# Gate products 6, 7 and 4 moved out of the attention heads into one PSUM bank per column behind them

## The chip, the core and the metric

The kernel runs on one core of a Trainium2 chip. A core has a matrix engine (PE, its weight loads shown as PEld), a vector engine (DVE), a scalar engine (ACT), GpSimd (POOL), a queue engine (SP), and 16 DMA engines which they all feed. Matmuls write to PSUM, eight banks of 128 partitions x 512 floats; everything else works in SBUF. The metric is the device time in microseconds of one execution; lower is better.

## The reference

One layer of an encoder on a sequence of 1024 tokens of width 1024, in float32:

```
h     = rmsnorm(x) * g_mix
z     = h @ w_in                         # 512 pooling channels | q | k | v
y_pool = pool_mixer(z[:, :512])          # windows 2, 4, 8, 16; per-group 128x128 map
y_attn = diff_attention(q, k, v)         # 8 heads, two softmax maps each
gates  = sigmoid(h @ w_gate + b_gate)    # 1024 x 2048
merged = gates[:, :1024] * (y_pool @ w_branch_pool) + gates[:, 1024:] * (y_attn @ w_branch_attn)
x = x + merged @ w_out
x = x + square(relu(rmsnorm(x) * g_ffn @ w_up)) @ w_down
```

The change concerns `h @ w_gate`: where its matmuls run, and how their results reach memory.

## The kernel before

**Exact float32 from split operands.** Each operand of a matmul is split into a high part (an ACT cast, line 136) and a low part (a subtraction on DVE or POOL, line 137). `mm3` (lines 140 to 145) multiplies high x high, high x low and low x high into one bank, so every product is three matmuls.

**Stages.** Setup and the norm of x; then the heads (a loop over `g`, lines 1024 to 1049); then the rest of the gates; then the pooling branch (`bp`, `branch_pool`), the attention branch (`ba`), `w_out` (`oX`, `oY`, `oZ`), and the MLP.

**The heads.** A turn `g` handles one tile of 128 tokens in each of nine stages, each some turns behind the one before (`ORDER`): A is q, k and v (`z`, 24 matmuls of 384 columns), B their norms, C the transposes of q and k (`tk`), D the scores, exponentials and the weighted difference (`sc`, `s`, `cf`), E the transpose of the probabilities (`ta`, `AT`), F the product with v (`po`), H and R the output norm, W the next head's weights. There are 64 tiles, 8 for each of 8 heads, and `g` runs on for ten more turns while the last stages drain.

**The fillers.** Matmuls that don't depend on the heads are mixed in as fillers. `fillers()` (line 489) walks through `G_PLAN` (line 51) and yields after each piece with its size in units. Line 1048 calls it until `made` reaches `F_UNITS` = 62 or `(g - 4) * 1.03`. What is left is issued behind the loop (line 1051). The pieces are:
- U, a pooling group: `h @ w_in` for 128 channels (`u`), the trailing sums on DVE, and the group's map (`yp`).
- A, B, 6, 4, 7: the gates.
- tB, t6, t4, t7: `t_set`, which prepares the second operands of products 5, 6, 4 and 7.
- A dot: an empty unit.

**The gates as Strassen's products.** `h @ w_gate` is cut into quarters and computed in Winograd's form of Strassen's algorithm, with seven products instead of eight. A product is done for one of eight blocks of 128 columns at a time: 4 blocks of the inner dimension x 3 matmuls of 512 columns, 12 matmuls. Its first operand is a column block of `w_gate` or of a sum of its quarters (`gw_sum`, made in memory by `gate_sums` with copies and accumulating DMAs at the turns of `G_SUMS`). Its second is a half of the transposed `h` (products 1, 2, 3) or a sum of quarters of it (`T`, products 5, 6, 7, 4). A piece A does products 1 and 2 in one bank, B does 5 and 3, and 6, 4, 7 are single.

`gate_unit` (line 465) loads the weights (`gate_weights`: a raw tile `frg` of a pool of two, split into `fwg`), does the matmuls, copies the bank with ACT after each product (`go`, lines 478 and 480) and sends the copy to those of the four quarters of `gd[c]` that it belongs to (`G_TO`). Products 1 and 2 are stored from ACT's queue (line 485); the others are added by an accumulating DMA from POOL's queue (line 487). Later `gate()` (line 236) loads the quarters for the sigmoid.

`t_set` (line 418) loads the two quarters of `h` (lines 435 and 436), subtracts on DVE (line 437) and splits into four tiles `T`. All four sets share the same four tiles; the fifth product's differences are also stored (`t2_dram`), and an accumulating DMA turns them into the operand of product 6.

**What sets the order.** The program states the order of its instructions; a scheduler of the language orders each engine's queue from it by priority and a modelled timeline when the kernel is built, within the tile slots that are free. At run time each queue is worked off in that order. `tc.issue_after(ins)` puts instructions behind `ins` on its engine.

**Room.** `ps_f` has one bank (`fill_bank`); behind the loop the gates take one of three (`spare_bank`). `up` has 11 slots `U`, which hold K, V, the scores and the probabilities, and later operands `yT` of the attention branch. `hp0` holds the first half of the transposed `h` (`hT`), `hp1` the second; `wpool` the heads' weights.

Of the kernel before, what the change touches and what calls it, by code (L numbers as in the profile page):

```python
# [49 lines left out]
F_FROM, F_PACE, F_UNITS = 4, 1.03, 62  # L50
G_PLAN = "A A A U A U A U A U A A . tB B B B B B B B B . t6 6 6 6 6 6 6 6 6 . t4 4 4 4 4 4 4 4 4 . t7 7 7 7 7 7 7 7 7"
G_SUMS = {
    9: "h0", 10: "i0 c1", 11: "h1", 12: "i1 a10", 13: "a11", 14: "h2", 15: "i2 c2", 16: "h3", 17: "i3 c3", 18: "a20",
    19: "a21", 20: "h4", 21: "i4 a30", 22: "a31", 23: "h5", 24: "i5 c4", 25: "h6", 26: "i6 a40", 27: "a41", 28: "h7", 29: "i7",
}
G_TO = {"1": (1, 4), "2": (0, 1), "6": (1, 4), "7": (2, 4), "5": (2, 3), "3": (1, 2), "4": (3, 4)}
# [12 lines left out]
def encoder_kernel(  # L69
# [248 lines left out]
    def fill_w(src, c0, name):  # L318
        ws = []
        for j in range(2):  # L320
            rw = fr_tile([P, 4, P], f"fr{name}_{j}")
            nc.sync.dma_start(
                rw, src[j * 512 : (j + 1) * 512, c0 : c0 + P].rearrange("(kk p) c -> p kk c", p=P)
            )
            w = fw_tile([P, 2, 4, P], f"fw{name}_{j}")
            split(w[:, 0], w[:, 1], rw, nc.gpsimd)
            ws.append(w)
        return ws

# [21 lines left out]
    def pool_group(g):  # L351
        win = WINDOWS[g]
        ws = fill_w(w_in, g * P, f"pool{g}")
        rg = fr_tile([P, P], f"rgrp{g}")
        nc.sync.dma_start(rg, w_pool_grp[g])
        wg = fq.tile([P, 2, P], F32R, tag="wg", name=f"wgrp{g}")
        split(wg[:, 0, :], wg[:, 1, :], rg, nc.gpsimd)
        u = fu_tile(f"u{g}")
        for th in range(2):
# [23 lines left out]
            split(m[:, 0, :], m[:, 1, :], cur[:, n0:n])  # L383
            yield
# [6 lines left out]
    def gate_sums(what):  # L391
# [14 lines left out]
        elif what[0] == "c":  # L406
            src = (None, wq(1, 0), gw_sum["1"], wq(1, 0), gw_sum["2"])[n]
            with tc.issue_after(marks["SP"]):
                nc.sync.dma_start(gw_sum[what[1]], src)
        else:  # L410
            src = (None, wq(1, 1), wq(0, 0), wq(0, 0), wq(0, 1))[n]
            r = slice(int(what[2]) * 256, int(what[2]) * 256 + 256)
            with tc.issue_after(marks["POOL"]):
                nc.gpsimd.dma_start(gw_sum[what[1]][r, :], src[r, :], accum_op=ALU.add, max_dma_last_dim=1024)
# [3 lines left out]
    def t_set(j):  # L418

        for k in range(4):  # L420
            if k < 2:
                t = fq.tile([P, 2, 512], F32R, tag=("fu", "mx")[k], name=f"T{j}_{k}")
            else:
                t = fwpool.tile([P, 2, 512], F32R, tag="fT", name=f"T{j}_{k}", bufs=N_FW // 2)
            T[j, k] = t
            rows = slice(k * P, (k + 1) * P)
            rw = raw([P, S], f"rT{j}_{k}")
            a, b = rw[:, 0:512], rw[:, 512:S]
            if j == "6":
                nc.sync.dma_start(a, t2_dram[rows, :])  # L430
            else:
                sa, sb = {
                    "5": (h_dram[0][0], h_dram[0][1]), "7": (h_dram[1][1], h_dram[0][1]), "4": (t2_dram, h_dram[1][0]),
                }[j]
                nc.sync.dma_start(a, sa[rows, :])
                nc.sync.dma_start(b, sb[rows, :])
                nc.vector.tensor_tensor(a, a, b, op=ALU.subtract)
            if j == "5":
                nc.sync.dma_start(t2_dram[rows, :], a)
            split(t[:, 0, :], t[:, 1, :], a)  # L440
        if j == "5":
            nc.gpsimd.dma_start(t2_dram, h_dram[1][1], accum_op=ALU.add, max_dma_last_dim=1024)
# [3 lines left out]
    def gate_weights(j, c):  # L446
# [8 lines left out]
        rw = fr_tile([P, 4, P], f"frg{j}_{c}")  # L455
        with ExitStack() as later:
            if n < 6:
                later.enter_context(tc.issue_after(h_hi[n // 2 + 2].ins))
                later.enter_context(tc.issue_after(loads["x3"].ins))
            marks["SP"] = nc.sync.dma_start(rw, src[r0 : r0 + 512, c0 : c0 + P].rearrange("(kk p) c -> p kk c", p=P)).ins  # L460
            w = fw_tile([P, 2, 4, P], f"fwg{j}_{c}")
            split(w[:, 0], w[:, 1], rw, nc.gpsimd)
        return w

    def gate_unit(js, c):

        ws = [gate_weights(j, c) for j in js]
        ps = (spare_bank if in_tail[0] else fill_bank)(f"g{js}_{c}")
        for n, (j, w) in enumerate(zip(js, ws)):
            for k in range(4):  # L470
                if j in "123":
                    b = [hT[k // 2 + 2 * (j != "1"), int(j == "3"), hl][:, k % 2, :] for hl in range(2)]
                else:
                    b = pair(T[j, k])
                mm3(ps, w[:, 0, k, :], w[:, 1, k, :], *b, k == 0 and n == 0, k == 3, n > 0)
            fo = fo_tile(f"go{j}_{c}")
            if j == "6":
                nc.scalar.activation(fo[:, 0:512], ps, AF.Copy, scale=-1.0)
            else:
                nc.scalar.copy(fo[:, 0:512], ps)  # L480
# [3 lines left out]
            if j in "12":  # L484
                nc.scalar.dma_start(dst, from_)
            else:
                nc.gpsimd.dma_start(dst, from_, accum_op=ALU.add)  # L487
# [1239 lines left out]
```

## Time and profile before

| | |
|---|---|
| median of 3 runs | 1548.94 us (1548.9 to 1551.23) |
| the profiled execution | 1553.23 us, of which the span from first to last instruction is 1551.5 us |
| granted PE clock over the span | 0.992 |
| instructions | 21873 |
| matmuls | 7542 |

Times below are from one profiled execution. A group is a line of the kernel, an engine, an operation, output <- inputs by their names without buffer numbers, and a count; behind it stand the busy time, the mean of one in ns, and the engine's idle time ahead of it with what ended that. PE's busy times come from matmuls whose ends are modelled. The chain that ended last can be followed back only to 823.8 us, where it begins with an instruction whose release the profile doesn't show; so for the heads and the gates PE's idle times and their releasers are used, and not this chain.

The page's slices show where the stages lie. Each digit is the busy share of one fortieth of the span, 38.8 us, in tenths:

```profile
PE   9999999999999999979999999999999999999999
POOL 4435355442636353445966420000000000000000
PEclk9999999999999999989999999999999999999999
DMA  7867687262434467589963733545442789637650
```

The heads fill the first 17 slices, the eighteenth and nineteenth hold the end of the heads and the remaining gates.

### The profile page before, as it was taken

How to read it: one execution, taken by the hardware profiler on the slowest of the kernel's cores; microseconds unless marked ns; L12 is line 12 of the kernel's file. 1: busy time of each engine (PE TensorE's matmuls, PEld its weight loads, DVE VectorE, ACT ScalarE, POOL GpSimd, SP SyncE). 2: the span in 40 equal slices, each digit the busy share in tenths (PEclk: the TensorE clock that was granted, in tenths of full speed). 3: DMA queues.
4: the chain of work that ended last, by engine and by line, in shares of the span. 5: the costliest groups of instructions: out<-in, count | busy, mean ns of one | idle time of the engine just before them, and what ended most of it. 6: DMA issues, size and time to landing. Idle time of an engine off the chain costs nothing. (4 is left out here: it accounts for less than half of the span.)

```text
span 1551.5 us, 21873 instructions
## 1 busy us (share of the span) xinstructions
PE 1516.4 (98%) x7542; PEld 1303.3 (84%) x7542; DVE 1069.1 (69%) x2101; ACT 829.2 (53%) x1717; POOL 460.5 (30%) x484
## 2 busy tenths in 40 slices
PE   9999999999999999979999999999999999999999
PEld 8899898989898989857888787888888878888887
DVE  7677767776867767764764799776666578546672
ACT  7666566565656656653553368566555544333331
POOL 4435355442636353445966420000000000000000
PEclk9999999999999999989999999999999999999999
DMA  7867687262434467589963733545442789637650
GB/s 228 295 115 218 138 170 142 71 201 71 107 62 96 86 147 139 134 214 280 360 210 121 260 143 101 164 165 188 150 142 109 255 314 367 217 122 256 225 191 27
DMA packets 210457, 271.43 MB, mean 175 GB/s; under 512 B 12037, under 2 KB 127466, under 8 KB 210282
## 3 DMA queue, kind: packets, MB, share of 16 engines
q1 hardware_dynamic: 172810, 212.32, 41.3%
q0 software_dynamic: 20368, 30.41, 13.4%
q10 hardware_dynamic: 17168, 27.31, 4.8%
q8 instruction: 59, 0.97, 0.3%
q14 instruction: 52, 0.43, 0.1%
HBM read 186.08 MB, written 101.74 MB: 186 GB/s over the span
## 5 line engine op out<-in xcount | busy, mean ns | idle before, releaser
L143 PE MATMUL z<-wqkv,hT 128*128 128x384 f32 x512 | 173.7, 340 | 1.1 <-ACT wqkv L136 0.8
L145 PE MATMUL z<-wqkv,hT 128*128 128x384 f32 x512 | 174.7, 341 | 0.0
L144 PE MATMUL z<-wqkv,hT 128*128 128x384 f32 x512 | 173.6, 339 | 1.0 <-POOL wqkv L137 1.0
L884 ACT ACTIVATE s<-s,nm 128x256 f32<-128x256 f32 (+7 forms) x128 | 99.5, 778 | 69.0 <-DVE nm L876 68.1
L807 POOL TENSOR_TENSOR ms<-ms,mhalf 128x4 f32<-128x4 f32 x64 | 69.9, 1092 | 166.9 <-DVE ms L806 162.4
L143 PEld LDWEIGHTS z<-wqkv,hT 128*128 128x128 f32 x512 | 96.5, 189 | 5.2 <-ACT wqkv L136 1.3
L144 PEld LDWEIGHTS z<-wqkv,hT 128*128 128x128 f32 x512 | 96.5, 189 | 5.1 <-POOL wqkv L137 2.0
L145 PEld LDWEIGHTS z<-wqkv,hT 128*128 128x128 f32 x512 | 96.5, 189 | 3.1 <-DVE hT L534 0.5
L137 POOL TENSOR_TENSOR fwg<-frg,fwg 128x512 fp32r<-128x512 f32 x56 | 88.5, 1581 | 29.5 <-ACT fwg L136 21.2
L876 DVE CUSTOM_DVE_ANT_0 s<-sc,dist 128x512 f32<-128x512 f32 (+3 forms) x128 | 74.2, 584 | 14.1 <-PE sc L874 11.8
L873 PE MATMUL sc<-K,Q 128*128 128x512 f32 (+2 forms) x192 | 69.2, 363 | 2.4 <-DVE Q L844 1.6
L874 PE MATMUL sc<-K,Q 128*128 128x512 f32 (+2 forms) x192 | 66.3, 350 | 0.0
L137 DVE TENSOR_TENSOR AS<-s,AS 128x512 fp32r<-128x512 f32 x64 | 43.4, 687 | 32.1 <-ACT AS L136 32.1
L487 POOL DMA_DIRECT2D gd<-go x40 | 43.0, 1076 | 71.3 <-ACT go L480 44.3
L137 POOL TENSOR_TENSOR wqkv<-rqkv,wqkv 128x384 fp32r<-128x384 f32 x56 | 60.5, 1178 | 10.5 <-ACT wqkv L136 6.9
L143 PE MATMUL g<-T,fwg 128*128 128x512 f32 x128 | 52.4, 412 | 4.7 <-ACT fwg L136 3.8
L145 PE MATMUL g<-T,fwg 128*128 128x512 f32 x128 | 52.6, 411 | 1.3 <-POOL fwg L137 1.2
L144 PE MATMUL g<-T,fwg 128*128 128x512 f32 x128 | 52.1, 407 | 0.8 <-DVE T L137 0.8
L929 PE MATMUL ta<-identf,s 128*128 128x128 f32 x288 | 45.6, 273 | 6.1 <-DVE s L893 5.6
L144 PE MATMUL ba<-yT,wba 128*128 128x512 f32 x128 | 49.9, 391 | 0.4 <-DVE yT L137 0.4
L137 POOL TENSOR_TENSOR wo<-ro,wo 128x512 fp32r<-128x512 f32 x28 | 41.0, 1480 | 28.7 <-ACT wo L136 27.3
L145 PE MATMUL ba<-yT,wba 128*128 128x512 f32 x128 | 49.3, 389 | 0.0
(498 smaller groups left out, 4874.4 us busy)
## 6 DMA issues: line engine op xcount, KB each, us to landing
wd<-in_w_down_dram SPq DMA_DIRECT2D x56, 512.0 KB, 5.5
wu<-in_w_up_dram SPq DMA_DIRECT2D x32, 512.0 KB, 5.4
udS<-us SPq DMA_DIRECT2D x64, 256.0 KB, 3.1
ur<-udS SPq DMA_DIRECT2D x32, 512.0 KB, 3.3
rqkv<-in_w_in_dram SPq DMA_DIRECT2D x64, 192.0 KB, 3.6
ur<-ud SPq DMA_DIRECT2D x24, 512.0 KB, 5.3
gw_sum<-in_w_gate_dram POOLq DMA_DIRECT2D x8, 1024.0 KB, 13.2
frg<-gw_sum SPq DMA_DIRECT2D x32, 256.0 KB, 3.9
```

The source lines that it names most:

```text
L137: (lo_eng or nc.vector).tensor_tensor(lo, src, f(hi), op=ALU.subtract)
L143: nc.tensor.matmul(ps, lhs_hi, rhs_hi, start=first, stop=False, **kw)
L144: nc.tensor.matmul(ps, lhs_hi, rhs_lo, start=False, stop=False, **kw)
L145: return nc.tensor.matmul(ps, lhs_lo, rhs_hi, start=False, stop=last, **kw)
L487: nc.gpsimd.dma_start(dst, from_, accum_op=ALU.add)
L807: marks["POOL"] = nc.gpsimd.tensor_tensor(ms, ms, mhalf[:, 0:4], op=ALU.pow).ins
L873: nc.tensor.matmul(dst, Q[:, i, 0, :], rhs, start=True, stop=False)
L874: nc.tensor.matmul(dst, Q[:, i, 1, :], rhs, start=False, stop=True)
L876: nc.vector.tensor_tensor_reduce(out=s[i][:, c : c + w], in0=sc[:, 0:w], in1=dist[:, o0 + c : o0 + c + w], scale=2.0 ** -(h + 1), scalar=B ...
L884: nc.scalar.activation(s[i][:, 0:n], s[i][:, 0:n], AF.Exp, bias=last, scale=-1.0, accum_out=Z[:, i, t : t + 1])
L929: nc.tensor.transpose(ta[:, i * P : (i + 1) * P], a[:, (4 * j + i) * P : (4 * j + i + 1) * P], identf)
```

## The change

- **Fillers** are now only the pooling groups, A and B. `F_UNITS` goes from 62 to 42 and `F_PACE` from 1.03 to 0.72. Each unit's raw weights are loaded one unit ahead; casts stand behind the last exponential (`held("ACT")`). The map of a pooling group is split later.
- **Gate sums** are made at other turns; the plain copies are cut into halves.
- **T operands.** Those of product 5 are prepared over six turns from turn 41 (`t1_set`), each loaded one turn before its subtraction. Those of 6, 7 and 4 are loaded at turn 61 into eight tiles of `hp0` and made in the turns from 64 on (`t_sets`), each in tiles of its own. DVE's steps stand behind the last `cf` of the heads (`held("DVE")`).
- **`last_gates`**, behind the loop and the rest of the B units, does 6, 7 and 4 for two columns at a time: one bank for each column accumulates the three products one after another. After each, DVE adds what `gd[c]` held in the quarter it belongs to (loaded before) to the bank's state, and ACT's queue stores the sum. Raw weights use four buffers, split ones six.
- `G_TO` of 1 stores to quarters 1, 2 and 3 as before; only 5 and 3 are accumulated by DMA.

The core of the diff:

```diff
-F_FROM, F_PACE, F_UNITS = 4, 1.03, 62
-G_PLAN = "A A A U A U A U A U A A . tB B B B B B B B B . t6 6 6 6 6 6 6 6 6 . t4 4 4 4 4 4 4 4 4 . t7 7 7 7 7 7 7 7 7"
+F_FROM, F_PACE, F_UNITS = 4, 0.72, 42
+G_PLAN = "A U A U A U A U A A A A B B B B B B B B"
...
-G_TO = {"1": (1, 4), "2": (0, 1), "6": (1, 4), "7": (2, 4), "5": (2, 3), "3": (1, 2), "4": (3, 4)}
+G_TO = {"1": (1, 4), "2": (0, 1), "5": (2, 3), "3": (1, 2)}
+T1_FROM, T_FROM = 41, 61
...
+    def t1_set():
+
+        rws = {}
+        for step in range(6):
+            k = step - 1
+            if 0 <= k < 4:
...
+                rw = rws.pop(k)
+                a, b = rw[:, 0:512], rw[:, 512:S]
+                with held("DVE"):
+                    nc.vector.tensor_tensor(a, a, b, op=ALU.subtract)
+                nc.sync.dma_start(t2_dram[k * P : (k + 1) * P, :], a)
+                split(t[:, 0, :], t[:, 1, :], a)
+            if step < 4:
+                rw = rws[step] = raw([P, S], f"rT5_{step}")
+                for i in range(2):
+                    nc.sync.dma_start(rw[:, i * 512 : (i + 1) * 512], h_dram[0][i][step * P : (step + 1) * P, :])
+            if step == 5:
+                with held("POOL"):
+                    nc.gpsimd.dma_start(t2_dram, h_dram[1][1], accum_op=ALU.add, max_dma_last_dim=1024)
+            yield
+
+    def t_sets():
+
+        rws = []
+        for k in range(4):
+            rows = slice(k * P, (k + 1) * P)
+            for srcs in ((t2_dram, h_dram[1][0]), (h_dram[1][1], h_dram[0][1])):
+                rw = htile([P, S], F32, f"rT{k}", 0)
+                for i in range(2):
+                    nc.sync.dma_start(rw[:, i * 512 : (i + 1) * 512], srcs[i][rows, :])
+                rws.append(rw)
+        for _ in range(3):
+            yield
+        for j in "674":
+            for k in range(4):
+                if j == "7":
+                    t = w_tile([P, 2, 512], f"T{j}_{k}", 1)
+                else:
+                    t = htile([P, 2, 512], F32R, f"T{j}_{k}", 1)
...
+                with held("DVE"):
+                    if j == "6":
+                        with held("ACT"):
+                            nc.scalar.activation(hi, a, AF.Copy, scale=-1.0)
+                        nc.vector.scalar_tensor_tensor(lo, a, -1.0, f(hi), op0=ALU.mult, op1=ALU.subtract)
+                    else:
+                        nc.vector.tensor_tensor(b, a, b, op=ALU.subtract)
+                        split(hi, lo, b)
+            yield
...
+    def split_unit(w, c, rws):
+        ws = []
+        for i, rw in enumerate(rws):
+            wt_ = fw_tile([P, 2, 4, P], f"fw{w}{c}_{i}")
+            with held("ACT") if "ACT" in marks else nullcontext():
+                split(wt_[:, 0], wt_[:, 1], rw, nc.gpsimd)
+            ws.append(wt_)
+        return ws
...
+    def last_gates():
+
+        nw = [0]
+
+        def raw_tile(shape, name):
+            if nw[0] % 4 < 2:
+                return fr_tile(shape, name)
+            return fo_tile(name)[:, 0:512].rearrange("p (a b) -> p a b", a=4)
+
+        def weights(j, c):
+            rw = gate_raw(j, c, raw_tile)
+            nw[0] += 1
+            w = (w_tile if nw[0] % 6 < 4 else lambda s, n, i: fwpool.tile(s, F32R, tag="fw", name=n, bufs=N_FW // 2))(
+                [P, 2, 4, P], f"w{j}_{c}", 0
+            )
+            split(w[:, 0], w[:, 1], rw, nc.gpsimd)
+            return w
+
+        for c0 in range(0, NK, 2):
+            cs = (c0, c0 + 1)
+            ps = {c: spare_bank(f"gX_{c}") for c in cs}
+            kept = {}
+            for c in cs:
+                b2, b1 = ut([P, 2, 512], F32, f"gk{c}"), ut([P, 512], F32, f"gl{c}")
+                nc.sync.dma_start(b2, gd[c][1:3].rearrange("q p t -> p q t"))
+                nc.sync.dma_start(b1, gd[c][3])
+                kept[c] = {"6": b2[:, 0, :], "7": b2[:, 1, :], "4": b1}
+            for j in "674":
+                for c in cs:
+                    gate_matmuls(ps[c], j, weights(j, c), j == "6")
+                    k = kept[c][j]
+                    nc.vector.tensor_tensor(k, ps[c], k, op=ALU.add)
+                    nc.scalar.dma_start(gd[c]["674".index(j) + 1], k)
...
+        t1_prep, t_prep = t1_set(), t_sets()
         units, made = fillers(), 0
...
+            if g >= T1_FROM:
+                next(t1_prep, None)
+            if T_FROM <= g < T_FROM + 5:
+                next(t_prep, None)
...
         in_tail[0] = True
         for _ in units:
             pass
+        for _ in t_prep:
+            pass
+        last_gates()
+        fw_all[0], fwcount[0] = True, 0
```

More of the change, by code (lines that the diff above doesn't have):

```diff
@@ L315, in alloc_T @@
         }
[L318 to L328, printed above, removed]
     nb = [0]
@@ L416, in encoder_kernel @@
[L416 to L442 removed]
+            dst, src = gw_sum[what[1]][r, :], pairs[what[0]][n - 1][r, :]
```

124 lines of the change are left out of this document (72 added, 52 removed), and 3 rows, old and new, of the table G_SUMS.

## The prediction

> **What bounds the kernel now.** I read the page's busy times first, then PE's busy time by stretches, then PE's list of waits for the worst stretch, then DVE's and SP's. The columns of the stretches are: stretch, its length, busy time and instruction count of PE, weight loads, DVE, ACT and POOL, granted PE clock, DMA share, GB/s.
>
> ```profile
> PE 1516.4 (98%) x7542; PEld 1303.3 (84%) x7542; DVE 1069.1 (69%) x2101; ACT 829.2 (53%) x1717; POOL 460.5 (30%) x484
> ```
> ```profile
> 80.00:122.00 42.00, 42.00 (x250) 39.15 (x249) 33.88 (x102) 25.02 (x61) 13.92 (x17) 1.00 0.65 119
> 125.00:475.00 350.00, 344.96 (x1989) 315.29 (x1988) 263.81 (x713) 208.87 (x530) 164.02 (x191) 1.00 0.55 128
> 475.00:535.00 60.00, 57.81 (x331) 52.20 (x331) 45.05 (x130) 37.31 (x93) 23.95 (x27) 1.00 0.41 93
> 560.00:583.00 23.00, 19.47 (x104) 17.45 (x103) 12.36 (x34) 11.23 (x29) 9.22 (x11) 0.93 0.67 144
> 583.00:633.00 50.00, 49.85 (x297) 46.25 (x296) 36.44 (x110) 29.48 (x74) 17.62 (x18) 1.00 0.61 132
> 633.00:665.00 32.00, 31.83 (x170) 27.06 (x170) 24.52 (x71) 24.09 (x57) 18.88 (x24) 1.00 0.75 157
> 665.00:700.00 35.00, 26.41 (x112) 19.80 (x111) 24.08 (x39) 17.60 (x35) 15.03 (x13) 0.80 0.90 219
> 700.00:725.00 25.00, 23.90 (x106) 18.91 (x105) 11.24 (x13) 10.57 (x21) 17.79 (x14) 1.00 1.02 253
> 725.00:770.00 45.00, 43.73 (x190) 35.59 (x191) 25.93 (x19) 22.06 (x38) 36.01 (x23) 1.00 1.03 371
> 770.00:870.00 100.00, 100.00 (x442) 82.77 (x442) 61.31 (x71) 40.34 (x64) 62.45 (x44) 1.00 0.62 199
> ```
> PE is the bound: it is idle for 1551.5 - 1516.4 = 35.1 us in all. So a change that keeps every matmul can win only from these 35 us and from matmuls that ran at half clock. In the last row 442 matmuls of 512 columns fill 100 us without a hole: **226 ns each**, which I use as the price of one. A gate product of one column is 12 of them, 2.72 us.
>
> The loss isn't spread evenly. Stretch 560:583 is idle 23.00 - 19.47 = 3.5 us, and the clock 0.93 takes up to 0.07 x 23 = 1.6 us more: **5.1 us**. From 633 to 725 the idle time is 0.2 + 8.6 + 1.1 = 9.9 us, and the clock 0.80 in 665:700 takes up to 0.20 x 35 = 7.0 us: **16.9 us**. The 350 us of 125:475 lose only 5.0 us, 1.4%. PE's waits in 560:725 name the causes:
>
> ```profile
> PE ta L929 <- DVE s L893: 3.8, 2, 2.2
> PE g L143 <- ACT fwg L136: 3.8, 3, 2.0
> PE po L144 <- DVE AT_0l L137: 1.7, 2, 1.4
> PE g L145 <- POOL fwg L137: 1.2, 1, 1.2
> PE g L143 <- ACT T L136: 0.9, 1, 0.9
> PE g L144 <- DVE T L137: 0.8, 1, 0.8
> ```
> Either the gates' own weights (fwg) and T operands are late, or DVE is late for the heads (s, AT). The second has the same origin: the T differences of line 437 stand in DVE's queue and wait for their loads.
>
> ```profile
> L437 DVE TENSOR_TENSOR rT<-rT x12: 676/692/741, 323.6 to 672.9; 128x512 f32<-128x512 f32 x12
> its engine sat idle before it (us, times) until:
>   DMA rT<-h_dram: 11.0, 6
>   DMA rT<-t_dram: 5.3, 1
> ```
> ```profile
> SPq L460 <- POOL fwg L137: 28.5, 9, 5.2
> ```
> DVE stood still for 16.3 us behind such loads. The last row is of SP's own waits in 633:725: SP waits 28.5 us for one of two raw weight buffers, with the next loads queued behind.
>
> **The change part by part.**
>
> *Matmuls.* Before there are 7 products x 8 columns = 56, or 672 matmuls. After there are 8 units of two products (1, 2), 8 of two (5, 3) and 24 single ones (6, 7, 4): again 56. **0 us.**
>
> *Where they run.* Before, 62 units less three empty ones leave 59 products inside the heads, 42 after. 17 x 2.72 = 46 us of matmuls move behind the heads, where 6 + 24 = 30 products (82 us) then lie. This costs nothing as long as PE stays full in the heads with less filler. The z row shows where the heads' main matmuls end:
>
> ```profile
> L145 PE MATMUL z<-wqkv,hT x512: 331/334/522, 9.1 to 634.4; 128*128 128x384 f32 x171
> ```
>
> They should end near 634 - 46 = 588 us. Does PE stay full? I counted the filler's matmuls (first two rows u, the rest g; stretch, length, PE busy and count):
>
> ```profile
> 80.00:122.00 42.00, 7.67 (x31) 1.00 0.65 119
> 125.00:475.00 350.00, 37.50 (x151) 1.00 0.55 128
> 125.00:475.00 350.00, 67.83 (x264) 1.00 0.55 128
> 475.00:535.00 60.00, 16.10 (x60) 1.00 0.41 93
> 583.00:633.00 50.00, 12.82 (x48) 1.00 0.61 132
> ```
> In 125:475 there are 415 of them, 34.6 products. At 1.03 per turn of the head loop that is 33.6 turns of 10.4 us, with 263.81 / 33.6 = 7.9 us of DVE each. The new pace of 0.72 takes 0.31 x 2.72 = 0.84 us out of a turn: 9.6 us, of which 2.0 us (21%) filler, and DVE at 7.9 / 9.6 = 82%. Such stretches are in the old trace already: 80:122 has 31 x 0.226 / 42 = 17% filler, DVE at 81% and no idle PE; 583:633 has 22% and loses 0.2 us; 475:535 has 23% and loses 2.2 us, 3.7%, the worst. The three together lose 2.3 of 152 us, 1.5%, like 125:475. So I take **+3 us** for the heads; the ends are 0 and, at the rate of 475:535 over 588 us, (3.7 - 1.4)% x 588 = +13.
>
> *T operands.* Product 5's are loaded one turn before their subtraction, and those of 6, 7 and 4 three turns before, about 29 us, each set into tiles of its own. The subtractions stand behind the turn's last small DVE step and should find their data landed. The stall of 560:583 goes: **-5 us**. What is late next there is nothing that the waits name.
>
> *The heads' tail.* Weights for the 24 products get four raw buffers instead of two and six split tiles, 16 us of matmuls ahead. The waits on fwg and T go, up to **-16.9 us** with the clock.
>
> *Out of the banks.*
>
> ```profile
> L480 ACT COPY go<-g 128x512 f32<-128x512 f32 x48 | 28.1, 586 | 27.2 <-PE g L145 19.1 <-DMA gd<-go 6.2 <-issue 1.3
> L487 POOL DMA_DIRECT2D gd<-go x40 | 43.0, 1076 | 71.3 <-ACT go L480 44.3 <-PE sc L874 10.8 <-PE ta L929 4.1
> L1147 DVE TENSOR_TENSOR mg<-ba,ga 128x512 f32<-128x512 f32 x16 | 10.8, 681 | 0.6 <-POOL mp L1056 0.6
> L137 POOL TENSOR_TENSOR fwg<-frg,fwg 128x512 fp32r<-128x512 f32 x56 | 88.5, 1581 | 29.5 <-ACT fwg L136 21.2 <-PE z L145 5.8 <-issue 1.5
> L136 ACT CAST fwg<-frg 128x512 fp32r<-128x512 f32 x56 | 34.7, 622 | 6.7 <-DMA frg<-in_w_gate_dram 4.2 <-DMA frg<-gw_sum 2.4
> L485 ACTq DMA_DIRECT2D gd<-go x16: 326/361/408, 36.2 to 354.1; - x16
> ```
> 24 of the 40 accumulating issues go: 24 x 1.076 = 26 us of POOL, and 24 ACT copies x 0.586 = 14 us. In their place come 24 DVE additions with one operand in a bank, 24 x 0.681 = 16 us by the nearest row (line 1147), 24 issues of a store on ACT, 24 x 0.361 = 9 us, and 16 loads on SP. In the 65 us of the 24 products PE sets the pace: POOL has 24 x 1.58 = 38 us of weights, ACT 24 x (0.62 + 0.36) = 24 us. POOL's 26 us I count at **0**: it was busy 164 of 350 us and no bound.
>
> The addition is a **new wait**. The next product of that bank can't start before it, and the other column's product covers 2.72 us. So DVE may come 2.72 - 0.68 = 2.0 us late for nothing. Behind the addition in DVE's queue stand the branch operands yT, behind the store in ACT's queue the next weights' casts, which the six tiles cover. DVE's neighbours there are the first two of these:
>
> ```profile
> L228 DVE SCALAR_TENSOR_TENSOR ryT<-ryT,gs,rb 128x512 f32<-128x512 f32 (+1 forms) x12 | 18.6, 1567 | 25.8 <-DMA rb<-r_dram 15.5 <-PE bp L145 5.2 <-DMA ryT<-y_dram 5.1
> L137 DVE TENSOR_TENSOR yT<-ryT,yT 128x512 fp32r<-128x512 f32 x16 | 19.3, 1244 | 5.0 <-ACT yT L136 5.0
> L137 DVE TENSOR_TENSOR T<-rT,T 128x512 fp32r<-128x512 f32 x16 | 10.9, 686 | 2.3 <-ACT T L136 2.3
> ```
> One of them is shorter than 2.0 us, two in a row aren't, by 0.8 us. I let that happen at five of 24, **+4 us** left of the tail's loss. The bounds are 0 and the second rival's.
>
> The Trainium skill speaks against this place: SBUF — State Buffer, section "SBUF: two separate sides", says that VectorE with two SBUF operands and GpSimd share a port pair that one holds for a whole instruction. The yT subtraction at 1244 ns beside a busy POOL, where the same form takes 686 ns on T (last row), fits that. By the page my estimate would be a POOL weight split of 1.58 us ahead of a neighbour more often, and +7 us instead of +4.
>
> *Bytes.*
>
> ```profile
> gd<-go POOLq DMA_DIRECT2D x24, 256.0 KB, 4.2
> gd<-go POOLq DMA_DIRECT2D x8, 768.0 KB, 7.7
> gd<-go POOLq DMA_DIRECT2D x8, 512.0 KB, 8.9
> ```
> Of these accumulations 16 of 256 KB stay; 12.6 MB go. In place come 6.3 MB of loads and 6.3 MB of stores. With 6.3 MB of weights the last 65 us carry 18.9 MB, 290 GB/s; 725:770 moved 371 with PE at 97%. The branch loads (up to 371 x 45 = 17 MB) may start earlier, because the heads' chain ends earlier relative to PE's work: 36 MB / 371 = 97 us, and from 588 there are 82 us of gates plus the pooling branch's 45. It fits, at **0**, if the queues spread it.
>
> *The rest.* The gate sums' copies in halves and at other turns move the same bytes on SP and POOL, four more issues; weights and pooling inputs are loaded a unit (2.8 turns) ahead and cast behind the last exponential; both hide in that lead: **0**.
>
> **Sum.** -5 - 16.9 + 4 + 3 = -15 us. The profiled execution took 1553.23 us (span 1551.5 and 1.7 around it), 0.3% above the median 1548.94. I subtract from the median: **1534 us**.
>
> **Rivals.**
>
> *The tail's starvation returns (same).* The 24 products' loads share SP with the branch loads, and a queue that waits in order did it in 665:700 at DMA share 0.90. For it: 28.5 us of SP's waits. Against: twice the buffers. Then the tail keeps its 16.9: 1549 - 5 + 3 = 1547 to 1549.
>
> *Heads short of filler.* If all heads lose like 475:535, +13 for +3: 1549 - 5 - 13 + 13 = 1544, on the edge of a difference. It decides when DVE's own waits, not its 82%, set the turn.
>
> *The additions wait in DVE's queue (slower).* Line 228 kept DVE waiting 25.8 us for rb, ryT and a pooling product. These steps can now stand ahead of an addition, and PE waits with them. From 2.0 us of lateness per addition on it costs: eight waits (5, 1 and 2) less 2.0 each give 10 us, uncovered 26, and the clock at 0.80 for 65 us another 13. With -19 for the rest it ends between 1549 - 19 + 10 + 13 = 1553 and 1549 - 19 + 26 + 13 = 1569; I take 1560. For it: DVE's queue is strict in the trace (it stood at line 437 with other work behind). Against: most of rb will have landed by then.
>
> A page makes this worse: the Trainium skill, TensorE: Matmul & The Clock Gate, "A second HAM failure mode: psum-queue depth-cycling", says that short stops at each change of bank can swing the clock to half. The pooling products of 725:770 change banks every 12 matmuls, 2.7 us, with clock 1.00, so the trace doesn't agree yet.
>
> *It doesn't do what it says:* the products could be put elsewhere in PE's order by the scheduler; the sum would be the same, with the stalls elsewhere.
>
> **Chances.** Forecast 0.60; starvation 0.10 (same); heads short 0.12 (half faster, half same); additions late 0.18 (slower). Differences below 0.2%, 3 us, can't be told from none here. Faster 0.66, same 0.16, slower 0.18. The range: below, the whole -22 with heads at 0 gives 1527, and a stall behind the gates may go too: 1525. Above, to 1556, so that of the slower case only its upper half is out.
>
> **What would show it.** Right: 560:583's kind of stall gone, no wait on line 437; z ending near 585 to 590; clock 1.00 through the tail; 24 products in about 65 us; waits of the new products on DVE below 5 us. Wrong: PE waiting for DVE's additions or for gd; heads that end after 600; more than 10 us of idle PE in the first 550 us.

## The result, and the profile after

The changed kernel took 1598.74 us (median of 4 runs, 1596.91 to 1600.97) beside 1550.09 us for the kernel before on the same chip: ratio 1.0306, 95% interval 1.0274 to 1.0338. That is 49 us slower where 15 us faster was forecast. The profiled execution has a span of 1597.3 us at a granted clock of 0.979.

The page's busy times, then PE's in the stretches of the prediction (columns as there):

```profile
PE 1535.2 (96%) x7542; PEld 1316.7 (82%) x7542; DVE 1055.1 (66%) x2125; ACT 818.9 (51%) x1693; POOL 426.9 (27%) x460
```
```profile
125.00:475.00 350.00, 334.76 (x1904) 307.35 (x1904) 260.71 (x722) 202.43 (x521) 146.95 (x177) 0.97 0.51 130
560.00:583.00 23.00, 23.00 (x136) 21.24 (x135) 14.20 (x42) 11.59 (x28) 8.39 (x8) 1.00 0.64 182
583.00:633.00 50.00, 43.44 (x251) 38.91 (x249) 40.21 (x121) 33.47 (x87) 11.56 (x18) 0.93 0.25 62
633.00:665.00 32.00, 21.49 (x84) 15.07 (x85) 25.73 (x61) 14.73 (x31) 5.94 (x6) 0.73 0.31 94
665.00:700.00 35.00, 25.73 (x112) 19.05 (x110) 8.86 (x16) 10.66 (x21) 23.07 (x20) 0.95 1.05 314
700.00:725.00 25.00, 19.57 (x72) 15.36 (x72) 8.11 (x10) 6.83 (x12) 21.68 (x18) 0.80 1.06 388
725.00:770.00 45.00, 45.00 (x200) 37.27 (x199) 14.53 (x20) 13.45 (x23) 23.57 (x19) 1.00 0.90 292
```
The same 7542 matmuls take 18.8 us more of busy time (a lower clock) with 27.0 us more of idle time. The loss has two places: 125:475 now loses 15.2 us at clock 0.97 (before 5.0 at 1.00), and 583:725 stands at 110.2 of 142 us. In 633:665 PE is at two thirds of its time and 0.73 of its clock while POOL does 6 us of work and the DMA engines 31%. No engine is full there (DVE, the busiest, has 25.7 of 32 us), so something waits. What was promised did come in 560:583, which is full, and in 725:770, where the new products run without a hole.

PE's waits in 600:725 of the changed kernel name the gates' weights above all (w and fwB), and between them the heads' last products (po):

```profile
PE gX L145 <- ACT w L138: 6.1, 3, 3.6
PE gX L147 <- POOL w L139: 5.8, 4, 3.0
PE po L1051 <- ACT oqs L138: 5.5, 2, 3.4
PE gB L145 <- ACT fwB L138: 4.6, 1, 4.6
```
Why a B unit's weights are late there is seen in the timelines of SP's queue and of ACT (start, length, engine and line, what, in brackets the idle time before it):

```profile
597.71 1.63 SPq L486 DMA_DIRECT2D frg<-gw_sum  x2
...
656.75 2.05 SPq L486 DMA_DIRECT2D frg<-gw_sum  x2
```
```profile
653.30 1.15 ACT L967 ACTIVATE s<-s,nm 128x1024 f32<-128x1024 f32 x1 [2.60 <-DVE nm L959]
...
654.44 1.12 ACT L138 CAST fwB<-frg 128x512 fp32r<-128x512 f32 x2
```
SP issued the two loads at 597.7 and the next ones at 656.8: for 57 us it could not refill the two raw buffers, since their cast stands at 654.44, directly behind the heads' very last exponential. The order is laid down by `held("ACT")` in `split_unit`. Inside the loop `marks["ACT"]` is the newest exponential; behind the loop it no longer moves, so every B unit left over is tied to the last one. The heads' chain meanwhile has nothing beside it, and the clock falls.

Inside the heads the same hold works in small. ACT, POOL and SP's queue around one unit:

```profile
436.84 1.15 ACT L967 ACTIVATE s<-s,nm 128x1024 f32<-128x1024 f32 x1
...
437.99 1.13 ACT L138 CAST fwA<-frg 128x512 fp32r<-128x512 f32 x2
```
```profile
438.67 3.95 POOL L139 TENSOR_TENSOR fwA<-frg,fwA 128x512 fp32r<-128x512 f32 x2
```
```profile
417.60 1.12 SPq L486 DMA_DIRECT2D frg<-in_w_gate_dram  x2
```
```profile
436.85 0.35 PE L956 MATMUL sc<-K,Q 128*128 128x256 f32 x1 [0.71 <-ACT AT_4h L138]
...
437.72 0.39 PE L956 MATMUL sc<-K,Q 128*128 128x256 f32 x1 [0.40 <-DVE nm L959]
...
440.45 0.79 PE L147 MATMUL gA<-hT,fwA 128*128 128x512 f32 x1 [1.07 <-POOL fwA L139]
```
The weights were asked for at 417.6 and cast at 438.0, behind the exponential that had just run. PE, in its fixed order, waited first for the scores with no filler to put in between, then for the filler itself. So PE's list of waits for 100:600 names the scores' chain (nm, s, oqs) and hardly the weights: the missing cover shows under other names. For the leads I took, from the trace, the time from the end of a unit's first cast to its first matmul, for the 18 units that start behind 80 us (the e-numbers are the experiments of the next section):

```
                                     first unit at   median lead   under 1 us
changed kernel                            58 us         2.4 us       7 of 18
  hold off in the tail (e1)               58 us         2.9 us       6 of 18
  hold from the fourth unit on (e13)      27 us         2.9 us       7 of 18
  the same, two turns older (e14)         26 us         4.3 us       3 of 18
  no hold, start in order (e9)            26 us        21.5 us       0 of 18
  no hold, no load ahead (e15)            27 us        22.0 us       0 of 18
```

### The profile page after: what moved, and what is told of

The parts are those of the page before. It is cut to its first block, busy times and chain, and to the rows that moved or that the text cites. A ratio compares the mean times of both kernels' runs of the same rounds, so it can differ in the third digit from the quotient of the medians.

```text
span 1597.3 us, 21921 instructions
## 1 busy us (share of the span) xinstructions
PE 1535.2 (96%) x7542; PEld 1316.7 (82%) x7542; DVE 1055.1 (66%) x2125; ACT 818.9 (51%) x1693; POOL 426.9 (27%) x460
## 4 chain that ended last, share of the span: by engine, by line
PE 67%; DVE 4%; DMA 2%; issue 2%; ACT 1%; POOL 1%; POOLq 0%; SPq 0%; ACTq 0%; DVEq 0%
PE Da L146 4%; PE Da L147 4%; PE Da L145 4%; PE Db L147 3%; PE Db L146 3%; PE Db L145 3%; PE X L145 2%; PE X L147 2%; PE X L146 2%; PE z L145 2%; PE z L146 2%; PE z L147 2%; PE ba L147 2%; PE ba L146 2%; PE ba L145 2%; PE Z L145 2%
## 5 line engine op out<-in xcount | busy, mean ns | idle before, releaser
L956 PE MATMUL sc<-K,Q 128*128 128x512 f32 (+2 forms) x192 | 72.6, 384 | 9.0 <-DVE nm L959 6.5
L957 PE MATMUL sc<-K,Q 128*128 128x512 f32 (+2 forms) x192 | 67.1, 361 | 0.0
L1014 PE MATMUL ta<-identf,s 128*128 128x128 f32 x288 | 50.4, 293 | 7.8 <-DVE s L978 3.7
L1014 PEld LDWEIGHTS ta<-identf,s 128*128 128x128 f32 x288 | 38.1, 151 | 16.3 <-DVE s L978 5.5
L956 PEld LDWEIGHTS sc<-K,Q 128*128 128x128 f32 x192 | 37.0, 194 | 16.5 <-DVE nm L959 10.3
L147 PE MATMUL ba<-yT,wba 128*128 128x512 f32 x128 | 49.8, 389 | 0.0
L145 PE MATMUL ba<-yT,wba 128*128 128x512 f32 x128 | 49.8, 389 | 0.0
L146 PE MATMUL ba<-yT,wba 128*128 128x512 f32 x128 | 49.8, 389 | 0.0
L138 ACT CAST AS<-s 128x512 fp32r<-128x512 f32 x64 | 39.0, 623 | 15.5 <-PE W L147 7.0
L139 DVE TENSOR_TENSOR A<-mp,A 128x512 fp32r<-128x512 f32 x28 | 28.6, 1031 | 26.1 <-ACT A L138 25.9
```

What stands on the lines that cost most here:

```text
L138: made = nc.scalar.copy(hi, src)
L139: (lo_eng or nc.vector).tensor_tensor(lo, src, f(hi), op=ALU.subtract)
L145: nc.tensor.matmul(ps, lhs_hi, rhs_hi, start=first, stop=False, **kw)
L146: nc.tensor.matmul(ps, lhs_hi, rhs_lo, start=False, stop=False, **kw)
L147: return nc.tensor.matmul(ps, lhs_lo, rhs_hi, start=False, stop=last, **kw)
L956: nc.tensor.matmul(dst, Q[:, i, 0, :], rhs, start=True, stop=False)
```

## The experiments

Theory H: the hold costs all of it. Theory D: less filler per turn leaves the heads bare. Unless said otherwise an edit is to the changed kernel; ratios are to the kernel before on the same chip, with 95% intervals. Three stretches of the kernel before, for comparison:

```profile
0.00:100.00 100.00, 97.02 (x548) 87.17 (x549) 73.72 (x199) 65.57 (x169) 46.15 (x79) 1.00 0.70 224
100.00:600.00 500.00, 489.24 (x2816) 447.47 (x2815) 371.77 (x1020) 299.48 (x752) 227.45 (x261) 1.00 0.57 126
600.00:725.00 125.00, 114.99 (x578) 96.21 (x576) 84.22 (x197) 70.86 (x160) 62.65 (x59) 0.95 0.80 189
```
and the last two of the changed kernel:

```profile
100.00:600.00 500.00, 482.04 (x2763) 443.55 (x2762) 368.91 (x1041) 293.33 (x749) 201.98 (x239) 0.98 0.49 123
600.00:725.00 125.00, 93.24 (x409) 71.97 (x408) 68.71 (x164) 54.18 (x120) 57.37 (x55) 0.85 0.64 199
```

**e1: no hold behind the loop.**

```diff
-            with held("ACT") if "ACT" in marks else nullcontext():
+            with held("ACT") if "ACT" in marks and not in_tail[0] else nullcontext():
```


> The changed kernel, but the casts of the gate units left over behind the loop no longer stand behind the last exponential. Theory H (the holds): behind the loop the mark no longer moves, so the last three B units wait for the heads' very last exponential (cast at 654 us, raw weights landed near 600). Freed, their 16 us of matmuls fill the hole of 612 to 650: 12 to 20 us less than the changed kernel, 1579 to 1587. Theory R (room and queues: slots, SP's order, T operands keep them late): within 4 us of the changed kernel's 1599.

1565.44 us, 1.0083 (1.0057 to 1.0110): 35 us off the changed kernel by the ratios.

```profile
100.00:600.00 500.00, 480.56 (x2758) 441.08 (x2757) 368.42 (x1040) 293.24 (x747) 201.65 (x239) 0.98 0.49 122
600.00:725.00 125.00, 115.34 (x562) 95.47 (x561) 78.91 (x180) 61.69 (x133) 56.92 (x55) 0.97 0.75 227
```
The tail has recovered to the level of before, and the heads are as they were. It is more than expected: the clock and the weights queued behind came back too.

**e2: no hold at all** (`with nullcontext():`).

> The changed kernel without any hold of weight casts behind an exponential. If the holds also cost the heads (theory H): matmul time lost before 600 us falls from about 59 us toward the 30 us of the kernel before, 1555 to 1570 in all. If the heads lose because less filler is mixed in (theory D, density): the heads lose 50 to 60 us as in the changed kernel, and the total is that of the run with a free tail, within 5 us.

1550.13 us, 0.9988 (0.9969 to 1.0006). In 100:600 PE is busy for 493.33 us at clock 1.00, more than before. But a new loss stands in the start, in ACT's timeline:

```profile
16.17 1.37 ACT L138 CAST fwA<-frg 128x512 fp32r<-128x512 f32 x2 [4.00 <-DMA frg<-in_w_gate_dram]
```
ACT waits 4.00 us for a filler's weights, with the start's casts queued behind. The kernel before kept these casts behind `h_hi` and the load of x3; in the changed kernel only the load is kept there, and the hold did the rest. So the hold was partly needed.

**e3: the kernel before at the new pace** (`F_PACE, F_UNITS = 0.72, 42`).

> The kernel before, with pace 0.72 and 42 units in the loop and nothing else of the change. Theory D: its heads lose like those of the changed kernel, the z matmuls end at 605 to 615 us, and the total is 1565 to 1600. Theory H: its heads lose no more than before (z ends at 585 to 595), and the total is 1540 to 1560, as the tail has more filler to cover its waits.

1586.24 us, 1.0204 (1.0154 to 1.0254), but not in the heads:

```profile
100.00:600.00 500.00, 491.41 (x2888) 455.50 (x2887) 379.57 (x1106) 307.88 (x785) 208.07 (x252) 0.99 0.45 106
600.00:750.00 150.00, 110.31 (x434) 80.95 (x433) 59.20 (x100) 57.78 (x113) 85.98 (x76) 0.86 0.98 239
```
With less filler PE is no emptier in the heads: 491.4 us busy for 489.2, at a clock 0.01 lower. Theory D falls. The tail is idle for 39.7 us, and its longest waits are for the T operands, one set of tiles for three products that follow each other, and for the gates' weights in two raw buffers:

```profile
PE g L143 <- ACT T L136: 11.6, 4, 5.2
PE g L143 <- ACT fwg L136: 11.1, 5, 8.8
```
The change has more room for both and keeps its new products full in 725:770. Which of its own sets, buffers and banks per column does that wasn't tested one by one.

**e4: the changed kernel with the old pace** (`F_PACE, F_UNITS = 1.03, 48`, `T1_FROM = 28`).

> The changed kernel at the old pace of 1.03, all 48 units in the loop, so that the filler ends near turn 51 and 13 turns have none. Theory D: the dense part loses like the kernel before (about 1.5% of its length), the turns without filler lose 2 us or more each, 25 us or more together; no B unit is left behind the loop, so part of the tail's hole can be filled by the last products. 1575 to 1600. Theory H: the dense part loses 5% as in the changed kernel.

1585.04 us, 1.0205 (1.0157 to 1.0252). More filler doesn't cure the heads while the hold is in them. The filler lasts to 536 us here, and up to 475 us PE is idle for 19.7 of 350 us (5.6%), where the kernel before at the same pace loses 5.0:

```profile
125.00:475.00 350.00, 330.32 (x1861) 300.75 (x1860) 243.45 (x680) 198.39 (x504) 155.10 (x179) 0.98 0.57 142
```

**e5: the hold in the kernel before, heads only.**

```diff
+            with tc.issue_after(marks["ACT"]) if "ACT" in marks and not in_tail[0] else nullcontext():
                 split(w[:, 0], w[:, 1], rw, nc.gpsimd)
```
The weights of the pooling groups get the same hold.

> The kernel before, with nothing of the change but the hold, and that inside the heads only: the casts and the subtractions of the filler weights go behind the newest exponential; plan, pace, tail and T sets stay those of before. Theory H (the hold itself starves the heads' fillers, since a weight is cast only after an exponential that comes late in the turn, while PE wants it early in the next): 10 to 25 us slower, 1560 to 1575, with the loss between 100 and 600 us and PE's idle time in the rows of gate weights ended by the casts. Theory L (the loss of 15 us between the changed kernel with the hold in the heads alone-out and with no hold needs the new loads a unit ahead, or the new order of units): within 4 us of the kernel before, 1546 to 1554.

1561.41 us, 1.0089 (1.0061 to 1.0116): the size fits H, the place doesn't.

```profile
0.00:100.00 100.00, 92.72 (x517) 83.97 (x518) 70.37 (x191) 61.27 (x161) 40.63 (x74) 0.98 0.54 171
100.00:600.00 500.00, 487.62 (x2794) 447.10 (x2793) 377.21 (x1013) 295.32 (x744) 227.72 (x260) 0.99 0.57 132
```
4.3 us of idle time are added up to 100 us and only 1.6 up to 600. The first unit's casts start at 55.0 us, where before had them at 24.9. So the price inside the heads isn't the same in both kernels, and was still open. (This execution's span is only 6.0 us above that of before, while the medians lie 12 us apart, so it shows about half of the loss.)

**e6, e7, e8: two places where e2 still loses.** e6 puts the first pair's kept products into raw buffers, e7 uses the plan "A A A U A U A U A U A A" again (with the loads of its first three units behind the start's marks), e8 does both.

```diff
-                b2, b1 = ut([P, 2, 512], F32, f"gk{c}"), ut([P, 512], F32, f"gl{c}")
+                b2 = raw([P, 2, 512], f"gk{c}") if c < 2 else ut([P, 2, 512], F32, f"gk{c}")
+                b1 = ut([P, 512], F32, f"gl{c}")
```


> The changed kernel without the hold, and the first pair's kept products (two tiles of 1024 columns) in the two raw buffers in place of U buffers that the heads hold until their last attention tile is done. Theory U (the 12 us that PE loses at 625 to 650 us come from loads of kept products that wait for a U buffer): 6 to 10 us off the run without the hold, 1540 to 1544, with the loads issued before 620 us. Rival W (the weights and the T sets are as late as the loads): within 3 us of it, 1547 to 1552, and the same stretch then shows PE waiting for ACT, POOL or DVE's casts.

> The changed kernel without the hold, and the early units in the order of before (three units of two stored products ahead of the first group of the pooling branch, their six loads behind the start's marks as before). Theory S (7 of the 8 us lost up to 25 us come from the loads and casts of the first pooling group, which stand among the start's own): 5 to 9 us off the run without the hold, 1541 to 1545, with the loss up to 25 us back at 1 to 2. Rival P (the start's loss comes from the pace and is only moved, since the heads are short of ready units at 62 to 75 us anyway): within 3 us of it, 1547 to 1552.

> Both of the last two edits on the changed kernel without the hold. If theories U and S are right and the two places are apart in time, their gains add up: 11 to 19 us off, 1531 to 1539, faster than the kernel before by 0.7 to 1.2 per cent and in the range of the prediction. If the freed time is given back in the tail (the last pairs end on the same transfers, or the clock is lowered as PE's density grows): 1542 to 1548.

e6: 1547.04 us, 0.9989 (0.9975 to 1.0003); e7: 1545.76, 0.9973 (0.9959 to 0.9987); e8: 1549.66, 1.0010 (0.9997 to 1.0023). None of the three gains came as expected; e6 came out as its rival W has it. e7's start is as slow as e2's (the first unit, not the pooling group, stands in it). In e6 the loads came early, and the next in line was the set of product 4, as DVE's timeline shows:

```profile
648.26 0.22 DVE L976 SCALAR_TENSOR_TENSOR cf<-cf,Z,nlam 128x1 f32<-128x1 f32 x1
...
648.61 2.49 DVE L466 TENSOR_TENSOR rT<-rT 128x512 f32<-128x512 f32 x4
```
It is the same fault on another engine: `held("DVE")` around this set is reached behind the loop, where its mark is the last `cf`.

**e9: e2 with the start put right.** The first three units' casts go behind the start's `h_hi` and the load of x3, as before.

```diff
+                if n < 3:
+                    later.enter_context(tc.issue_after(h_hi[n + 2].ins))
+                    later.enter_context(tc.issue_after(loads["x3"].ins))
                 split(wt_[:, 0], wt_[:, 1], rw, nc.gpsimd)
```
**e10: e6 with the set of product 4 free. e11: all of these together. e12: e11 with the plan "A A U A U A U A U A A A".**

```diff
-                with held("DVE"):
+                with held("DVE") if j != "4" else nullcontext():
```


> The changed kernel without the hold, but with the weights' casts of the first three units behind the start's own columns of h and the last early load of x, where the kernel before has them. The trace of the run without the hold shows ScalarE at 12.4 to 16.2 us waiting 4.0 us for a filler's weights with the start's casts behind it in its queue, and PE idle 4.5 us. Theory Q (that queue is the start's whole loss): slack up to 25 us goes from 11.9 back to about 5, and the clock granted at 16 to 22 us with it; 5 to 8 us off the run without the hold, 1541 to 1545. Rival P (the unit stands in the start at all, whatever its casts): within 2 us of it, 1548 to 1552.

> The run without the hold and with the first pair's kept products in raw buffers, and the set of product 4 no longer held behind the newest factor of the heads: in that run its subtractions start at 648.6 us, 0.1 us behind the last tile's factor, though its rows and slots were there long before. Theory T (the tail's remaining loss at 638 to 654 us is the same fault, a mark that no longer moves): 4 to 7 us off the run with raw buffers (1547), so 1540 to 1543, and the set made before 640 us. Rival B (the scores' chain itself leaves PE idle there, with the tail's products short of banks or of weights): within 2 us, 1545 to 1549.

> All of these: no hold in the heads and the tail, the first three units' casts behind the start, the set of product 4 free, raw buffers for the first pair. If theories Q and T hold and their places are apart in time: 1533 to 1539, the range's lower half of the prediction and faster than the kernel before by 0.7 to 1.1 per cent. If the gains are given back, as those of the two earlier edits were: 1542 to 1547.

> The same with the early units as A A U A U A U A U A A A, so that a second stored unit and not a pooling group is at hand when the first scores wait at 62 to 75 us. If the 5 us lost there come from the missing filler and nothing later pays for it: 2 to 5 us off the run with all edits, 1530 to 1536. If a later stretch pays (as at 375 us with three stored units first, which lost 3.7 us there): within 2 us of it.

e9: 1536.2 us, 0.9905 (0.9892 to 0.9918). e10: 1540.38, 0.9933 (0.9921 to 0.9945), 0.56% below e6. e11: 1530.78, **0.9867 (0.9849 to 0.9885)**. e12: 1539.16, 0.9924 (0.9910 to 0.9937). Theories Q and T hold, e9 with more than expected (13 us off e2 for 5 to 8), and in e11 they add up, to a little less than the 1533 to 1539 expected. e12's order of units costs 8 us; that a unit more at 62 us would help was wrong, and why the order matters so much stays open. e9:

```profile
100.00:600.00 500.00, 493.67 (x2898) 457.18 (x2897) 384.99 (x1099) 308.95 (x792) 211.26 (x254) 1.00 0.50 121
600.00:725.00 125.00, 117.11 (x534) 94.69 (x533) 69.95 (x135) 51.58 (x101) 68.66 (x56) 0.96 0.88 299
```
e11, the page's first line, then the tail:

```profile
PE 1505.4 (99%) x7542; PEld 1301.3 (85%) x7542; DVE 1056.1 (69%) x2125; ACT 816.1 (53%) x1693; POOL 427.1 (28%) x460
```
```profile
600.00:725.00 125.00, 120.96 (x570) 99.48 (x569) 68.09 (x129) 56.64 (x111) 74.69 (x60) 1.00 0.94 313
```
It is faster than both kernels: PE is idle for 1527.9 - 1505.4 = 22.5 us in all.

**e13 to e15: why the hold costs in the heads.** All start from e9. e13 puts the hold back from the fourth unit on, inside the loop; e14 the same behind an exponential two turns older; e15 has no hold, but loads each unit's weights when the unit begins.

```diff
+                elif not in_tail[0]:
+                    later.enter_context(held("ACT"))                  # e13
+                    later.enter_context(tc.issue_after(exps[-5]))     # e14
```
**e16: e11 with the sets of 6 and 7 free too.**

> The run with the start put right and no hold (1536), with the hold put back inside the heads alone, from the fourth unit on. Theory H (the hold alone takes the heads' time): 18 to 28 us above it, 1554 to 1564, all of it between 100 and 600 us, with the granted clock below 1.00 there. Rival S (the difference of 29 us between the changed kernel with a free tail and the run without a hold came from the start and from the scheduler's other order): 1536 to 1545.

> The same, but with the hold behind an exponential two turns older than the newest. Theory M (it is the mark: the newest exponential is one that ScalarE reaches only when the unit's matmuls are wanted, and an older one has long run): within 5 us of the run without a hold, 1533 to 1542. Rival A (any order laid on ScalarE's queue costs, since casts, exponentials and copies then wait on each other): over 10 us above it, 1546 or more.

> The run with the start put right and no hold, but each unit's raw weights loaded when the unit begins, as in the kernel before, and not a unit ahead. Theory M (the lead is what keeps PE fed in the heads, and the hold spoils the lead): slower than with the lead by 5 to 20 us, 1541 to 1556, in the heads and, by the B units that are left, in the tail. Rival N (the lead is worth nothing, as the scheduler puts loads early anyway where a buffer is free): within 4 us, 1532 to 1540.

> The fastest version so far (1530.8), with the sets of products 6 and 7 also free of their marks. If these marks too are late for PE: 2 to 4 us off, 1527 to 1529. If they are not, or if freed subtractions now wait for loads in VectorE's queue ahead of the heads' own work, as those of the kernel before did: 1531 to 1540.

e13: 1552.91 us, 1.0012 (1.0000 to 1.0023), 17 us above e9, a little less than expected; of the 18.0 us between the two profiled executions 9.4 are busy time at a lower clock, 8.6 idle time, and 5.8 of the idle time lie in 100:600. e14: 1534.26, 0.9895 (0.9879 to 0.9910). e15: 1536.36, 0.9904 (0.9891 to 0.9918). e16: 1531.44, 0.9872 (0.9858 to 0.9885), level with e11. 100:600 in e13 and in e14:

```profile
100.00:600.00 500.00, 487.91 (x2830) 449.12 (x2830) 375.03 (x1067) 298.80 (x766) 206.70 (x246) 0.99 0.48 119
```
```profile
100.00:600.00 500.00, 494.38 (x2902) 457.73 (x2901) 386.92 (x1102) 312.17 (x797) 217.48 (x256) 1.00 0.49 121
```
The hold as such is free (e14); what costs is that its mark is the newest exponential. How much of the cost goes through the lead of the table isn't settled: e14's median is only 1.4 us above e13's, with 3 units under 1 us for 7. That the program states the loads a unit ahead makes no difference (e15): without it they are issued within 5 us of e9's all the same, and the leads of the two are alike, as rival N has it.

The hold's price, at 1550 us, from the ratios: in the tail 1.0306 - 1.0083 = 2.2%, 35 us; on the first three units, 1.0083 - 1.0012 = 0.7%, 11 us; in the rest of the heads 1.0012 - 0.9905 = 1.1%, 17 us. The intervals of the four ratios leave some 6, 4 and 3 us of doubt in these. Together they are 62 us, and what is left of the change is 0.9905, 15 us faster. Each price is that of one hold with the others as they stood in these runs. With the hold the first unit starts at 58 us instead of 27, but most of the 11 us are not lost there: in 100:600 PE is busy for 480.56 us in e1 and 487.91 in e13. Why the first three units tell so late wasn't followed.

## The prediction, step by step

**The step that failed** is the one under "The rest": weights "are loaded a unit (2.8 turns) ahead and cast behind the last exponential; both hide in that lead: 0". I took the lead of the load for a lead of the cast. The cast's place is set by its mark, so the lead left was 2.4 us, not 2.8 turns; and behind the loop the mark stands still, so the B units left over waited 57 us for their buffers. In place of 0 it measured 62 us. I named what stands behind the additions in their queues, and didn't ask the same of the casts.

**The sum without it came out, in part by luck.** e9 is the change without this hold, with the first three units' casts where the kernel before has them: 0.9905 of 1548.94 is 1534.2 us for a forecast of 1534. But the time was won elsewhere than I had put it. Of the 18.0 us between the profiled executions of before and e9, 11.1 are idle time and 6.9 busy time at a higher clock. Of the idle time 4.4 us went in 100:600, only 2.1 in 600:725, and 4.5 in 725:900, to which the sum gave nothing (the range alone names a stall behind the gates). PE's clock rose there too. The stretch before, and in e9:

```profile
725.00:900.00 175.00, 170.49 (x736) 139.93 (x737) 108.54 (x113) 76.73 (x131) 116.82 (x78) 0.98 0.70 234
725.00:900.00 175.00, 175.00 (x782) 145.06 (x781) 109.47 (x141) 85.56 (x152) 99.04 (x68) 1.00 0.59 193
```
Term by term:
- *T operands, -5.* The stall is gone as forecast: 560:583 is full.
- *Heads, +3.* Better: the heads of e9 are idle for 6.3 us in 100:600, where before had 10.8; the stall above is among these 4.4. No price for less filler is left to be seen, and the rival "heads short of filler" is refuted by e3 too. The z row of e9, where I had an end at 588 us:

```profile
L147 PE MATMUL z<-wqkv,hT x512: 331/334/525, 9.6 to 583.0; 128*128 128x384 f32 x171
```
- *Tail, -16.9.* Too much for the change as built: 600:725 is idle for 7.9 us at clock 0.96 in e9, for 10.0 at 0.95 before. Only e11, with two more faults mended, has it: 4.0 us at 1.00. Product 4's set and the kept products' buffers were not in my sum.
- *Additions, +4, and the slower rival.* Wrong in the mechanism. In the changed kernel DVE waits for PE's products, not PE for DVE, as their group shows:

```profile
L589 DVE TENSOR_TENSOR gk<-gX,gk 128x512 f32<-128x512 f32 x16 | 11.0, 690 | 44.9 <-PE gX L147 44.9
```
  In 725:770 PE has no hole beside them. With the hold gone from the tail PE does wait for an addition: 4.3 us in e1, 1.3 us in e9.

```profile
PE gX L145 <- DVE gk L589: 4.3, 1, 4.3
```
  That is about the size of my +4, but not its cause: it is the first addition of all, in e1 its kept product was loaded late (issued at 664.5 us, and DVE's own last wait was for it), and no step of the branches stood ahead of it. That the result came out slower doesn't bear this rival out: 1599 us is 30 above its upper end of 1569, and its cause was not there.
- *The Trainium skill on DVE and POOL* (SBUF — State Buffer, "SBUF: two separate sides") stood behind my dearer estimate for the additions' neighbours. The additions themselves have one operand in PSUM, so the page's rule on two SBUF operands doesn't reach them, and they took 690 ns. The yT steps have two, and their median went from 1213 ns before to 685 ns after:

```profile
L137 DVE TENSOR_TENSOR yT<-ryT,yT x16: 679/1213/1855, 684.6 to 780.3; 128x512 fp32r<-128x512 f32 x16
```
```profile
L139 DVE TENSOR_TENSOR yT<-ryT,yT x16: 679/685/1191, 767.6 to 805.3; 128x512 fp32r<-128x512 f32 x16
```
  The trace of before agrees with the page: ten of its sixteen yT steps began while an instruction of POOL was running and took 836 to 1855 ns, the other six met none and took 679 to 692 ns. After, one step of sixteen is long (1191 ns), and it too began beside such an instruction. Once POOL came second there: its step took 2.88 us behind three yT steps of 682 to 686 ns, for 1.29 us in those just before. The +7 us that I drew from this were not borne out: in e1 and e9 no branch step stood ahead of the addition that PE waited for.
- *"Tail's starvation returns"* was the nearest rival in kind (PE waits for weights), but by another road and at twice its price, 35 us for 16.9.

Of the signs that I named, the two for "wrong" that came true, heads ending after 600 (their last z matmul starts at 614.3 us) and over 10 us of idle PE in the first 550, said which step: neither belongs to the tail's additions.

## What to carry to other kernels

Ask of every ordering hint what its mark is at the moment when the instruction is queued: the newest instruction of a chain is a late one, and a mark that is set in a loop stands still behind it. Here a mark two turns older cost nothing. When the engines' waits name a chain's own latency, look for the filler that should have been beside it, and take the time from when its operands were ready to when they were used.

## What the runs showed of the hardware

The clock falls without any long hole. In the heads of the changed kernel, around the unit above:

```profile
435.89:439.30 3.41, 2.12 (x11) 1.18 (x9) 3.34 (x17) 3.31 (x7) 1.64 (x2) 1.00 0.00 0
439.30:446.13 6.83, 5.75 (x17) 4.61 (x17) 6.19 (x10) 2.89 (x10) 3.32 (x2) 0.50 0.56 180
```
PE was busy for 2.12 of 3.41 us (62%), with no single wait over 0.71 us, and the next 6.83 us ran at 0.50. In these PE was busy for 5.75 us, which at half clock lost 2.9 us, beside the 2.4 us of waiting around them. So here several waits of about a microsecond or less, close together, cost more than twice their sum. The Trainium skill (TensorE: Matmul & The Clock Gate, "What's actually happening") has the half rate follow an idle window of about 3.4 us. The length agrees with this trace; idle the window was not.

The 18 traces of this case show where the limit lies. In each of them the half clock comes and goes on a grid of 3.41 us. A stretch of that grid at full clock with PE busy for less than 44% of it was always followed by the half clock, and one with more than 67% never; between the two it went either way (78 falls of the clock, without the first 12 and the last 4 us of each trace).

That page's second rule in the prediction ("A second HAM failure mode: psum-queue depth-cycling") is about short stops at changes of bank. In 725:770 the new products change banks every 12 matmuls, at clock 1.00, but without a stop: PE is busy for 45.00 of 45.00 us. So a change of bank alone does nothing here, and the page's case, with stops, is not shown by this stretch.
